# Ordering the second half of the last output product and the first products of a feed-forward as written

## The chip, the cores and the metric

The kernel runs on one core of a Trainium2 chip. A core has a matrix engine (TensorE: PE in the profile, its weight loads PEld), a vector engine (VectorE: DVE), a scalar engine (ScalarE: ACT), GpSimd (POOL) and a queue that issues DMAs (SP). Each takes its own instructions one after the other and waits for the others by semaphores. The metric is the device time of one execution in microseconds (us); less is better.

## The reference

One layer of a hybrid decoder, for 1024 tokens of width 1024, in float32. What matters here is its end:

```python
mixed = gates[:, :, 0] * y_ssm + gates[:, :, 1] * y_conv + gates[:, :, 2] * y_attn
x = x + mixed @ w_out[i]
h = rms_norm(x, ffn_norm_g[i])
f_gate, f_up = jnp.split(h @ ffn_w_gate_up[i], 2, axis=-1)
x = x + (jax.nn.silu(f_gate) * f_up) @ ffn_w_down[i]
```

`rms_norm` divides each token's row by the root of the mean of its squares and multiplies by a gain per column. `ffn_w_gate_up` is 1024 x 5632.

## The kernel before

Every product in float32 is made of three matmuls in the engine's faster float32 type: an operand is split into a high part (ACT copies it, L61) and the rest (DVE subtracts, L62), and high x high, high x low and low x high are added up in PSUM. On top of that the large products here use a Strassen scheme: 2 x 2 blocks and seven products in place of eight, with sums and differences of blocks as operands.

`out_rows` (from L1256) computes `mixed @ w_out` and adds it to x. Its seven products run in the order of `OUT`; each has four k-steps (`i`) and four token tiles (`t`), and one k-step of one tile is three matmuls (`mm`, L1282). A finished sum in PSUM is added to the tile's page x2 by DVE (`into`, L1290). The last product, number 4, is handled apart (from L1326): its loop has the tiles outside and the k-steps inside, and after each tile it finishes rows. `row` (L1294) takes one tile of 128 tokens: the sum of its squares (ACT, L219), the root (ACT, L209), the reciprocal (DVE, L210), the scaling (ACT for `act`, L213, else DVE, L215), and a DMA that keeps x2 in DRAM (L1297). Rows 0 to 3 are done during product 7, rows 4 to 7 here.

`quadrants` (L1364) turns four normalised rows into four blocks of 128 columns x 512 tokens: 16 transposes on PE (L1373) into two wide PSUM buffers, and four evictions, by ACT with the gain (L1379) or, where another operand is subtracted, by DVE (L1377). `operand_b` (L1393) splits such blocks. These are the right operands of the feed-forward's seven products: "11" and "21" come from rows 0 to 3, "T1" to "T4" and "22" need rows 4 to 7 too.

`ffn_up` (L1405) is a generator that yields at set places, so that `out_rows` can run it piece by piece with `next(up)`. Its list `flat` holds (i, z, p): a pair i of 128-column tiles of the weights, gate or up (z), the product p. It starts with products 1 and 2 of three pairs, which need right operands 11 and 21 alone. `operand(n)` splits the left operand of entry n from the raw weights (L61 and L62, tiles A), and for some entries starts the load of a later group (L1426). One product is twelve matmuls (L1517). Product 1 is copied from PSUM by ACT (L1520), and product 2 is added on top of it in the same bank:

```python
nc.tensor.matmul(ps, x, y, start=p in (1, 5, 6, 7) and k + j == 0, stop=k == 3 and j == 2,
```

After product 2 ACT applies SiLU for the gate (L1458), or DVE multiplies for the up part (L1462), from the same bank.

Which instruction stands where in an engine's queue is set by a planner: it walks through the program, lets each instruction in when its inputs, its tile's buffer and its engine are free by its own model of time, and gives the earlier one in the program the right of way. Inside `manual_schedule`, the named engines take their instructions in the order of the program. The kernel before uses that for PE in the state-space part alone (L1757); everything around the change is left to the planner. Buffers come from pools: 44 pages of 128 x 1024 floats, 14 of half that size, four PSUM banks and two wide PSUM buffers of two banks.

Of the kernel before, what the change touches and what calls it, by code (L numbers as in the profile page):

```python
# [12 lines left out]
OP = mybir.AluOpType  # L13
# [20 lines left out]
class Trunk:  # L34
# [554 lines left out]
    credit, t = 0.0, 0  # L589
# [666 lines left out]
    def out_rows(self):  # L1256
        nc = self.nc
        v = nc.vector
        x2, ss, xn = {}, self.const("ss2", [P, NT]), {}
        self.spill_x = self.dram.tile([S, D], F32, tag="sx", name="sx")  # L1260
        up = self.ffn_up()
        seq, parts = self.out_seq, {}

        def load(t):
            x2[t] = self.page("x2")
            nc.sync.dma_start(x2[t], self.i["x"][0, t * P:(t + 1) * P, :])

        def split(n):
            if n >= len(seq) or n in parts:
                return  # L1270
            p, i = seq[n]
            if n not in self.out_parts:
                self.out_right(n)
            r = self.left[i]
            if p in (1, 2):
                t = r.pop(p)
            else:
                t = self.page("lp", F32R)
                self.split(t[:, :512], t[:, 512:], r["src"].pop(p))
            parts[n] = t, self.out_parts.pop(n)  # L1280

        def mm(ps, n, t):  # L1282
            p, i = seq[n]
            act, w = parts[n]
            for j, (x, y) in enumerate(((0, 0), (0, 1), (1, 0))):
                nc.tensor.matmul(ps, act[:, x * 512 + t * P:x * 512 + (t + 1) * P], w[:, y * 512:y * 512 + 512],  # L1286
                                 start=i == 0 and j == 0 and p in (1, 5, 2), stop=i == 3 and j == 2,
                                 skip_group_check=True)

        def into(t, c, ps):  # L1290
            o = x2[t][:, c * 512:c * 512 + 512]
            v.scalar_tensor_tensor(o, ps, 0.5, o, op0=OP.mult, op1=OP.add)

        def row(t, act):  # L1294
            self.square_sum(x2[t], ss[:, t:t + 1])
            xn[t] = self.norm_row(x2[t], ss[:, t:t + 1], act)
            nc.sync.dma_start(self.spill_x[t * P:(t + 1) * P, :], x2[t])  # L1297
            del x2[t]
        INTO = {1: ((0, 0),), 2: ((0, 0),), 5: ((1, 1),), 6: ((0, 1),), 3: ((0, 1),), 7: ((1, 1),), 4: ((1, 0),)}
        for t in range(4):  # L1300
            load(t)
        first = [self.acc() for _ in range(4)]
        second = None
        for n, (p, i) in enumerate(seq[:-4]):
            if i == 0 and p in (5, 2):
                second = []
                for _ in range(2):
                    a = self.wide()
                    second += [a[:, :512], a[:, 512:]]
            if p == 2:  # L1310
                load(4 + i)
            for m in range(n, n + 3):
                split(m)
            for t in range(4):
                ps = (first if p in (1, 6, 7) else second)[t]
                mm(ps, n, t)
                if i == 3:
                    for h, c in INTO[p]:
                        into(4 * h + t, c, ps)
            del parts[n]  # L1320
            if p == 7 and i < 2:
                row(2 * i, 0)
                row(2 * i + 1, 0)
            if p == 7 and i == 0:
                next(up)
        n0 = len(seq) - 4  # L1326
        for n in range(n0, n0 + 4):
            split(n)
        self.B, half0 = {}, [xn.pop(j) for j in range(4)]
        q = self.quadrants(half0, 0)  # L1330
        for t in range(4):
            for n in range(n0, n0 + 4):
                mm(first[t], n, t)
            into(4 + t, 0, first[t])
            if t == 0:
                q += self.quadrants(half0, 4)
            elif t == 1:
                self.operand_b("11", q[:4])
                next(up)
            elif t == 2:  # L1340
                self.operand_b("21", q[4:])
            if t:
                row(3 + t, t % 2)
        row(7, 0)
        parts.clear()
        next(up)
        half1 = [xn.pop(4 + j) for j in range(4)]
        b11, b21 = q[:4], q[4:]
        t1 = self.quadrants(half1, 0, b11)
        self.operand_b("T1", t1)  # L1350
        next(up)
        b22 = self.quadrants(half1, 4)
        t2 = self.difference(v, b22, t1)
        self.operand_b("T2", t2)
        next(up)
        t3 = self.difference(v, t2, b11)
        self.operand_b("T3", t3)
        next(up)
        t4 = self.difference(v, b21, t2)
        self.operand_b("T4", t4)  # L1360
        self.operand_b("22", b22)
        self.run(up)
# [42 lines left out]
    def ffn_up(self):  # L1405

        nc = self.nc
        v = nc.vector
# [10 lines left out]
        def fetch(n):  # L1419
            if n < len(groups):  # L1420
                i, z, _ = groups[n]
                r = []
                for a in range(2):
                    t = self.page("raw")
                    c0 = z * D_FF + 2 * i * P
                    nc.sync.dma_start(t.rearrange("p (k c) -> p k c", k=4),  # L1426
                                      gu[4 * a * P:4 * (a + 1) * P, c0:c0 + 256].rearrange("(k p) c -> p k c", p=P))
                    r.append(t.rearrange("p (k f c) -> p k f c", k=4, f=2))
                raw[groups[n]] = r

        def operand(n):
            if n >= len(flat) or flat[n] in ops:
                return
            i, z, p = flat[n]
            g = i, z, int(i >= N or i > 0 and p not in (1, 2))
            if g[2] == 0 and p == 2 and i < N - 2:
                fetch(groups.index(g) + 4)
            elif p == 5:
                fetch(max(groups.index(g) + 2, 2 * N + z))
            lo, hi = raw[g]  # L1440
            a11, a21, a12, a22 = lo[:, :, 0], lo[:, :, 1], hi[:, :, 0], hi[:, :, 1]
            cut = lambda x: x.rearrange("p (k c) -> p k c", k=4)
            if p in (1, 2, 4):
                src = {1: a11, 2: a12, 4: a22}[p]
            else:
                src = cut(self.half("S"))
                x, y, op = {5: (a21, a22, OP.add), 6: (sums.get((i, z, 5)), a11, OP.subtract),
                            7: (a11, a21, OP.subtract), 3: (a12, sums.get((i, z, 6)), OP.subtract)}[p]
                v.tensor_tensor(src, x, y, op=op)  # L1449
                if p in (5, 6):  # L1450
                    sums[i, z, p] = src
            t = self.page("A", F32R)
            self.split(cut(t[:, :512]), cut(t[:, 512:]), src)
            ops[flat[n]] = t
# [32 lines left out]
            fetch(n)  # L1487
        yield
        for n in range(5):
            operand(n)  # L1490
        yield
        for n, (i, z, p) in enumerate(flat):
# [294 lines left out]
```

## Time and profile before

| | |
|---|---|
| three runs | 1752.97, 1753.34, 1754.22 us; median 1753.34 |
| the profiled execution's own time | 1753.43 us |
| its span, first to last instruction | 1751.5 us |
| granted TensorE clock, mean | 0.999 |
| transposes of the normalised rows (L1373) | 64, from 1086.5 to 1131.4 us |
| copies of product 1 (L1520) | 22, the first at 1107.6 us |

The span is shorter than the execution's own time by 1.9 us, which lie around it. The region that the change touches is that from 1086 to some 1158 us of the span.

### The profile page before, as it was taken

Reading aid. Unit: us, or ns where it says so; the run is one execution under the profiler, and the core shown is the slowest. Engines: PE = TensorE matmul, PEld = TensorE weight load, DVE = VectorE, ACT = ScalarE, POOL = GpSimd, SP = SyncE. Lnnn points to the kernel's source line nnn. Section 1 sums busy time; section 2 is a strip of 40 time slices with the busy share of each in tenths; the row PEclk is TensorE's granted clock in tenths of the full one; section 3 lists DMA queues with packets and bytes.
Section 4 is the critical chain, followed back from the end, with each engine's and each line's share of the span. In section 5 each row is a group of like instructions: output and inputs, shape, how many; then the busy total and the mean of one; then the engine's idle time right before and its main releaser. Section 6 shows DMA issues by size and latency. Waiting matters only on the chain.

```text
span 1751.5 us, 23611 instructions
## 1 busy us (share of the span) xinstructions
PE 1728.9 (99%) x8637; PEld 1433.2 (82%) x8637; DVE 1202.8 (69%) x2414; ACT 795.4 (45%) x1477; POOL 108.8 (6%) x94
## 2 busy tenths in 40 slices
PE   8999999999999999999999999999999999999999
PEld 8987788888888888888788888778888888888887
DVE  6975456667676664684685687798677776687681
ACT  7415566777777842333122244742222332344460
POOL 0000000000000010121000000011122111120000
PEclk9999999999999999999999999999999999999999
DMA  5213422221211125123566224333223332577521
GB/s 173 73 43 101 125 85 67 61 61 46 58 43 47 42 81 145 41 69 97 191 200 200 84 96 133 120 127 127 96 96 109 114 103 78 189 256 259 163 91 48
DMA packets 172664, 189.78 MB, mean 108 GB/s; under 512 B 16937, under 2 KB 129669, under 8 KB 172549
## 3 DMA queue, kind: packets, MB, share of 16 engines
q1 hardware_dynamic: 172517, 188.27, 33.5%
q8 instruction: 68, 1.11, 0.3%
q14 instruction: 47, 0.39, 0.1%
q10 hardware_dynamic: 32, 0.01, 0.0%
HBM read 134.50 MB, written 47.45 MB: 104 GB/s over the span
## 4 chain that ended last, share of the span: by engine, by line
PE 86%; DVE 6%; ACT 4%; issue 1%; DMA 1%; SPq 1%; POOL 0%; POOLq 0%; ACTq 0%; DVEq 0%
PE wide L1517 13%; PE acc L124 12%; PE acc L120 12%; PE acc L122 11%; PE acc L1517 9%; PE acc L1624 6%; PE wide L1624 5%; PE acc L560 3%; PE wide L519 3%; PE acc L1286 2%; PE wide L1286 2%; PE acc L583 2%; PE acc L582 2%; PE wide L257 1%; PE wide L256 1%
## 5 line engine op out<-in xcount | busy, mean ns | idle before, releaser
L120 PE MATMUL acc<-hh,whi 128*128 128x512 f32 x672 | 268.6, 400 | 1.5 <-DVE kl L66 1.5
L122 PE MATMUL acc<-hl,whi 128*128 128x512 f32 x672 | 267.9, 399 | 0.0
L124 PE MATMUL acc<-hh,wlo 128*128 128x512 f32 x672 | 267.4, 398 | 0.0
L1517 PE MATMUL wide<-B,A 128*128 128x512 f32 x1056 | 250.6, 391 | 0.3
L1517 PEld LDWEIGHTS wide<-B,A 128*128 128x128 f32 x1056 | 196.5, 188 | 47.0 <-DVE sg L1530 3.3
L1517 PE MATMUL acc<-B,A 128*128 128x512 f32 x792 | 190.6, 391 | 2.6 <-ACT A L61 1.6
L1517 PEld LDWEIGHTS acc<-B,A 128*128 128x128 f32 x792 | 147.9, 188 | 35.4 <-ACT A L61 2.5
L120 PEld LDWEIGHTS acc<-hh,whi 128*128 128x128 f32 x672 | 126.6, 188 | 22.3 <-issue 2.2
L122 PEld LDWEIGHTS acc<-hl,whi 128*128 128x128 f32 x672 | 126.7, 188 | 19.7 <-issue 0.2
L124 PEld LDWEIGHTS acc<-hh,wlo 128*128 128x128 f32 x672 | 126.8, 189 | 19.4 <-DVE wlo L62 0.4
L61 ACT ACTIVATE A<-S 128x512 fp32r<-128x512 f32 x88 | 54.8, 627 | 164.9 <-DVE S L1449 164.3
L62 DVE TENSOR_TENSOR ptl<-acc,pth 128x512 fp32r<-128x512 f32 (+1 forms) x152 | 93.8, 619 | 50.4 <-ACT pth L61 49.2
L1624 PE MATMUL acc<-wdp,act 128*128 128x512 f32 x528 | 121.5, 389 | 0.1
L524 DVE CUSTOM_DVE_ANT_0 p<-wide,mask 128x640 f32<-128x640 f32 (+7 forms) x128 | 90.1, 704 | 43.2 <-PE wide L519 40.5
L62 DVE TENSOR_TENSOR wlo<-raw,whi 128x1024 fp32r<-128x1024 f32 (+1 forms) x75 | 90.4, 1209 | 39.5 <-ACT whi L61 23.9
L1624 PEld LDWEIGHTS acc<-wdp,act 128*128 128x128 f32 x528 | 99.0, 188 | 21.2 <-DVE wdp L62 0.5
L1473 POOL TENSOR_TENSOR sg<-sg 128x512 f32<-128x512 f32 x44 | 73.9, 1679 | 590.3 <-ACT A L61 512.5
L527 ACT ACTIVATE p<-p,small 128x640 f32<-128x640 f32 (+7 forms) x128 | 93.6, 731 | 37.1 <-DVE small L524 35.1
L120 PE MATMUL acc<-mhi,whi 128*128 128x512 f32 x256 | 100.5, 392 | 1.8 <-DVE m L1166 1.8
L61 ACT ACTIVATE pth<-acc 128x512 fp32r<-128x512 f32 (+1 forms) x152 | 80.9, 534 | 46.0 <-PE acc L560 45.2
L124 PE MATMUL acc<-mhi,wlo 128*128 128x512 f32 x256 | 100.7, 393 | 0.3 <-DVE wlo L62 0.3
L122 PE MATMUL acc<-mlo,whi 128*128 128x512 f32 x256 | 100.5, 393 | 0.0
(397 smaller groups left out, 3246.1 us busy)
## 6 DMA issues: line engine op xcount, KB each, us to landing
raw<-in_ffn_w_gate_up_dram SPq DMA_DIRECT2D x52, 512.0 KB
raw<-in_w_in_dram SPq DMA_DIRECT2D x48, 512.0 KB
sa<-sg SPq DMA_DIRECT2D x77, 256.0 KB
araw<-sa SPq DMA_DIRECT2D x77, 256.0 KB
sg<-tg SPq DMA_DIRECT2D x48, 256.0 KB
gp<-sg SPq DMA_DIRECT2D x24, 512.0 KB
x<-in_x_dram SPq DMA_DIRECT2D x16, 512.0 KB
wd<-in_ffn_w_down_dram SPq DMA_DIRECT2D x11, 512.0 KB
```

What stands on the lines that cost most here:

```text
L61: self.nc.scalar.activation(hi, src, AF.Copy)
L62: self.nc.vector.tensor_tensor(lo, src, hi.bitcast(F32), op=OP.subtract)
L120: self.nc.tensor.matmul(out, hi(k), mh(k), start=start and j == 0, stop=False)
L122: self.nc.tensor.matmul(out, hi(k), ml(k), start=False, stop=False)
L124: self.nc.tensor.matmul(out, lo(k), mh(k), start=False, stop=stop and j == n - 1)
L519: nc.tensor.matmul(ps[:, c * 512:c * 512 + w], self.QS[t][:, h], k[:, k0 + c * w:k0 + c * w + w], start=z == 0, stop=z == 1)
L524: nc.vector.tensor_tensor_reduce(p[:, :n].rearrange("p (c w) -> p c w", c=pieces), v, m.rearrange("p (c w) -> p c w", c=pieces), scale=-1. ...
L527: nc.scalar.activation(p[:, :n], p[:, :n], AF.Exp, scale=-1.0, bias=st[:, hh:hh + 1], accum_out=st[:, 2 + hh:3 + hh])
L1286: nc.tensor.matmul(ps, act[:, x * 512 + t * P:x * 512 + (t + 1) * P], w[:, y * 512:y * 512 + 512], start=i == 0 and j == 0 and p in (1, 5, ...
L1473: e.tensor_tensor(o, x, y, op=op)
L1517: nc.tensor.matmul(ps, x, y, start=p in (1, 5, 6, 7) and k + j == 0, stop=k == 3 and j == 2, skip_group_check=True)
L1624: nc.tensor.matmul(ps, act[:, x * 512 + t * P:x * 512 + (t + 1) * P], w[:, y * 512:y * 512 + 512], start=i == 0 and j == 0 and p in (1, 5, ...
```

## The change

Three things change in the last product of `out_rows` and the start of `ffn_up`. The loop over the four tiles and what follows up to operand T1 stand in a `manual_schedule` for PE, DVE and ACT. Rows 5 and 7 take their sum of squares on DVE with one `tensor_tensor_reduce`; rows 4 and 6 keep ACT. And the order of the program is another: after the second tile come right operand 11, the left operands of entries 0 and 1, and right operand 21; after the third, rows 4 and 5; after the fourth, the left operands of entries 2 to 4, and rows 6 and 7. For this the generator yields once more, before entry 2. The loop that adds up products, its banks and the steps behind T1 stay as they were.

```diff
-        def row(t, act):
-            self.square_sum(x2[t], ss[:, t:t + 1])
+        def row(t, act, dve=False):
+            if dve:
+                v.tensor_tensor_reduce(self.page("junk"), x2[t], x2[t], scale=1.0, scalar=0.0, op0=OP.mult, op1=OP.add,
+                                       accum_out=ss[:, t:t + 1])
+            else:
+                self.square_sum(x2[t], ss[:, t:t + 1])
...
-        q = self.quadrants(half0, 0)
-        for t in range(4):
-            for n in range(n0, n0 + 4):
-                mm(first[t], n, t)
-            into(4 + t, 0, first[t])
-            if t == 0:
-                q += self.quadrants(half0, 4)
-            elif t == 1:
-                self.operand_b("11", q[:4])
-                next(up)
-            elif t == 2:
-                self.operand_b("21", q[4:])
-            if t:
-                row(3 + t, t % 2)
-        row(7, 0)
-        parts.clear()
-        next(up)
-        half1 = [xn.pop(4 + j) for j in range(4)]
-        b11, b21 = q[:4], q[4:]
-        t1 = self.quadrants(half1, 0, b11)
-        self.operand_b("T1", t1)
-        next(up)
+        E = mybir.EngineType
+        with self.tc.manual_schedule(engines={E.PE, E.DVE, E.Activation}):
+            q = self.quadrants(half0, 0)
+            for t in range(4):
+                for n in range(n0, n0 + 4):
+                    mm(first[t], n, t)
+                into(4 + t, 0, first[t])
+                if t == 0:
+                    q += self.quadrants(half0, 4)
+                elif t == 1:
+                    self.operand_b("11", q[:4])
+                    next(up)
+                    self.operand_b("21", q[4:])
+                elif t == 2:
+                    row(4, 1)
+                    row(5, 0, True)
+                else:
+                    next(up)
+                    row(6, 1)
+                    row(7, 0, True)
+            parts.clear()
+            next(up)
+            half1 = [xn.pop(4 + j) for j in range(4)]
+            b11, b21 = q[:4], q[4:]
+            t1 = self.quadrants(half1, 0, b11)
+            self.operand_b("T1", t1)
+            next(up)
...
         for n in range(5):
+            if n == 2:
+                yield
             operand(n)
```

## Rows read from the trace of the kernel before

**Rows 1.** The page's line of the span and its table of busy time by engine (us busy, share of the span, instructions).

```profile
span 1751.5 us, 23611 instructions
...
PE 1728.9 (99%) x8637; PEld 1433.2 (82%) x8637; DVE 1202.8 (69%) x2414; ACT 795.4 (45%) x1477; POOL 108.8 (6%) x94
```

**Rows 2.** The table of five stretches: busy us of PE, PEld, DVE, ACT and POOL, each with its number of instructions, then the granted clock, the share of the DMA engines and GB/s.

```profile
1086.46:1104.65 18.19, 18.09 (x94) 14.26 (x92) 14.40 (x24) 13.53 (x25) 0.00 (x0) 1.00 0.84 283
1104.65:1118.26 13.61, 13.61 (x62) 11.21 (x61) 5.64 (x11) 9.24 (x17) 0.00 (x0) 1.00 0.53 182
1118.26:1131.39 13.13, 10.92 (x62) 8.55 (x61) 10.80 (x18) 9.85 (x18) 0.00 (x0) 1.00 0.05 20
1131.39:1158.58 27.19, 25.55 (x111) 19.70 (x110) 26.88 (x46) 17.06 (x31) 0.00 (x0) 1.00 0.29 97
1158.58:1206.72 48.14, 48.14 (x214) 39.71 (x213) 41.80 (x58) 14.11 (x23) 9.54 (x6) 1.00 0.41 137
```

**Rows 3.** PE's instructions in order of time, 1074 to 1300 us, equal neighbours merged: start, us from the first's start to the last's end, engine, line, operation, output and input, shape, how many, and in brackets the idle time before and who ended it.

```profile
1086.46 0.60 PE L1373 MATMUL wide<-ident,xn 128*128 128x128 f32 x4
1086.82 3.00 PE L1286 MATMUL acc<-wop,lp 128*128 128x512 f32 x12
1089.66 0.60 PE L1373 MATMUL wide<-ident,xn 128*128 128x128 f32 x4
1090.02 3.82 PE L1286 MATMUL acc<-wop,lp 128*128 128x512 f32 x12
...
1097.09 0.66 PE L1373 MATMUL wide<-ident,xn 128*128 128x128 f32 x4
1097.50 0.48 PE L1286 MATMUL acc<-wop,lp 128*128 128x512 f32 x1
...
1104.65 13.77 PE L1517 MATMUL acc<-B,A 128*128 128x512 f32 x60
...
1120.27 0.44 PE L1373 MATMUL wide<-ident,xn 128*128 128x128 f32 x2 [1.20 <-DVE xn L215]
1121.71 3.08 PE L1517 MATMUL acc<-B,A 128*128 128x512 f32 x12 [1.00 <-ACT A L61]
...
1128.29 1.03 PE L1373 MATMUL wide<-ident,xn 128*128 128x128 f32 x8
...
1142.27 3.01 PE L1517 MATMUL acc<-B,A 128*128 128x512 f32 x12 [0.69 <-ACT p L1520]
...
1154.02 0.73 PE L1517 MATMUL acc<-B,A 128*128 128x512 f32 x2 [0.58 <-ACT A L61]
...
1156.18 2.56 PE L1517 MATMUL acc<-B,A 128*128 128x512 f32 x10 [0.38 <-DVE A L62]
```

**Rows 4.** ACT's instructions in the same form, 1070 to 1145 us.

```profile
1090.08 1.27 ACT L1379 ACTIVATE bq<-wide,gn 128x512 f32<-128x512 f32 x2 [0.95 <-PE wide L1373]
...
1107.57 0.60 ACT L1520 ACTIVATE p<-acc 128x512 f32<-128x512 f32 x1 [2.99 <-PE acc L1517]
...
1109.63 2.18 ACT L61 ACTIVATE B<-bq 128x512 fp32r<-128x512 f32 x4
1111.72 1.04 ACT L219 ACTIVATE junk<-x 128x1024 f32<-128x1024 f32 x1
1112.67 0.18 ACT L219 ACTIVATION_READ_ACCUMULATOR junk<-x 128x1 f32 x1
...
1113.24 0.28 ACT L209 ACTIVATE ss<-ss,eps 128x1 f32<-128x1 f32 x1
...
1115.12 1.15 ACT L213 ACTIVATE xn<-x,ss 128x1024 f32<-128x1024 f32 x1 [0.23 <-DVE ss L210]
```

**Rows 5.** One line of the source, L1373 (the transposes): how many, and the ns of one at least, in the middle and at most.

```profile
L1373 PE MATMUL wide<-ident,xn x64: 270/272/328, 1086.5 to 1131.4; 128*128 128x128 f32 x64
```

**Rows 6.** DVE's instructions in order of time, 1070 to 1145 us, in the form of rows 3.

```profile
1087.80 0.69 DVE L1292 SCALAR_TENSOR_TENSOR x<-acc,x 128x512 f32<-128x512 f32 x1 [3.23 <-PE acc L1286]
...
1095.28 0.68 DVE L62 TENSOR_TENSOR lp<-tgp,lp 128x512 fp32r<-128x512 f32 x1
...
1113.55 0.16 DVE L210 RECIPROCAL ss<-ss 128x1 f32<-128x1 f32 x1 [0.77 <-ACT ss L209]
1113.75 0.75 DVE L215 TENSOR_SCALAR xn<-x,ss 128x1024 f32<-128x1024 f32 x1
...
1123.58 1.40 DVE L1377 SCALAR_TENSOR_TENSOR bq<-wide,gn,bq 128x512 f32<-128x512 f32 x2
...
1126.60 2.49 DVE L62 TENSOR_TENSOR B<-bq,B 128x512 fp32r<-128x512 f32 x4
```

**Rows 7.** DVE's groups by line and shape: how many, then us in all and the mean ns of one, and the idle time before them. The first three are of the whole span, the last of 180 to 640 us, where the attention runs.

```profile
L62 DVE TENSOR_TENSOR wlo<-raw,whi 128x1024 fp32r<-128x1024 f32 x72 | 87.8, 1221 | 39.5 <-ACT whi L61 23.9 <-PE acc L122 10.7 <-ACT tg L672 2.5
...
L524 DVE CUSTOM_DVE_ANT_0 p<-wide,mask 128x1024 f32<-128x1024 f32 x8 | 9.8, 1224 | 3.9 <-PE wide L519 3.9
...
L62 DVE TENSOR_TENSOR mlo<-yT,mhi 128x1024 fp32r<-128x1024 f32 x4 | 8.1, 2029 | 2.0 <-ACT mhi L61 2.0
...
L524 DVE DVE_READ_ACCUMULATOR2_ANT small<- 128x1 f32 x128 | 10.6, 83 | 0.0
```

**Rows 8.** The issues on SP's queue in order of time, 1040 to 1145 us.

```profile
1079.66 8.80 SPq L1426 DMA_DIRECT2D raw<-in_ffn_w_gate_up_dram  x8
...
1100.53 2.61 SPq L1426 DMA_DIRECT2D raw<-in_ffn_w_gate_up_dram  x4
```

## The prediction

> **What bounds the kernel now.** I read the page first: TensorE (PE) is busy 99% of 1751.5 us, so only time in which PE stands still can be won, and any new stall of PE is paid in full [rows 1]. Then the table of stretches, to see where it stands still. The change touches about 1086 to 1158 us. PE has no idle time in the first two of these stretches beyond 0.1 us, 2.2 us in the third (13.13 less 10.92) and 1.64 us in the fourth, and afterwards it is dense (48.14 of 48.14 in the fifth) [rows 2]. So 3.85 us is all that shows as idle, and whatever delay or gain stands at 1158 us reaches the end. PE's order of time shows one more piece: twelve matmuls at 1090.02 took 3.82 us where twelve in a row take 3.00, so about 0.8 us is hidden there; with the 0.1 of the first stretch and small change I call it 0.65 to 1 [rows 3]. The ceiling of a gain is thus about 4.5 to 5 us, under 0.3%.
>
> The same view shows how the kernel fills PE today. Within L1286 and L1373, transposes stand in fours between matmuls, and 60 matmuls of the feed-forward's first five products run without a gap from 1104.65 [rows 3]. The code says why that is remarkable: product 2 adds to the same PSUM bank as product 1 (`start` is false for p == 2), so it can't begin before the copy of product 1 (L1520) has read the bank. The copy ran at 1107.57 for 0.60, when PE was inside the next product [rows 4]: the planner had put another product between. That such a wait is real is seen once at 1142.27, where PE stood 0.69 us for L1520 [rows 3].
>
> **The change, part by part.** The times below are on the clock of this profile. Unit prices: 60 matmuls in 13.77 us with a last one of 0.39 are 0.227 each, twelve 2.72; eight transposes in 1.03 with one of 0.27 are 0.11 each, sixteen 1.8 [rows 3, 5]. On DVE four splits in 2.49 with one of 0.68 are 0.60 apiece, and the sums into x2 (L1292) the same [rows 6]. On ACT four in 2.18 are 0.52 apiece [rows 4]. An eviction by ACT is 0.64, one by DVE 0.70 [rows 4, 6]. A hand-over between engines costs 0.03 (a root that ended at 1113.24 + 0.28 = 1113.52 was followed by its reciprocal at 1113.55 [rows 4, 6]); I use 0.04.
>
> (a) *Last output product as written.* PE must now run 16 transposes, then for the first sum all four k-steps, then 16 transposes, then the other three sums. Before, it took whichever step was split. The last pair's split ends on DVE at 1095.28 + 0.68 = 1095.96 [rows 6], so the first sum's last three matmuls run to 1095.96 + 0.68 = 1096.64. What follows is 1.8 + 36 x 0.227 = 9.96, to 1106.60, where before PE was through at 1104.65 [rows 3]: 1.95 us lost. From below: if the planner splits the pairs earlier, as ACT's halves would allow (DVE idles 3.23 us ahead of 1087.80 [rows 6]), nothing is lost and the hidden 0.65 comes back: -0.65. From above: one more pair of splits ahead of it, 2 x 0.60 late: +3.15. I take 1.95, since the splits are traced ahead of the block and nothing in it moves them.
>
> (b) *Vector queue as written, with two squares on it.* The second sum's addition (L1292) is now ahead of the right operands' splits in DVE's queue. It waits for PE: 1096.64 + 1.8 + 2.72 + 0.17 of pipeline = 1101.33. Behind it DVE never rests: addition 0.6, four B splits 2.4, two A 1.2, four B 2.4, addition 0.6 (7.2 so far); row 4's reciprocal 0.2, row 5's square 1.3, the wait for its root on ACT 0.4, reciprocal 0.2, scaling 0.7 (2.8); addition 0.6, three A 1.8 (2.4); row 6's reciprocal 0.2, row 7's square 1.3 (1.5). Sum 13.9, to 1115.25. Reciprocal and scaling are from their rows (0.16 and 0.75, 0.19 and 0.68 from start to next start) [rows 6]. The two-source reduction is in the trace for one PSUM and one SBUF source: 1224 ns for 128x1024 and 83 ns for its accumulator, 1.3 together [rows 7]. For two SBUF sources it is not shown; the nearest rows are 0.75 (the scaling of one source, [rows 6]) and 2.03 (a two-source instruction on a strided page, [rows 7]), which move the sum by -0.5 (one square is then hidden behind ACT) and by +1.5.
>
> (c) *ACT's queue.* The copy of product 1 is written behind row 7's root. ACT is ready for that root long before it comes: its own work from 1089 on is 8 evictions of 0.64, 13 splits of 0.52 and two rows of some 2.5 (square 1.04, accumulator 0.18, scaling 1.15), about 17 us, to 1106. But it can't pass it. Root at 1115.3, copy to 1116.05, product 2 from 1116.1. PE has ended product 1 at 1106.60 + 2.72 = 1109.32, so it stands 6.8 us. Queued behind the wait on PE are products 2 to 5, T1's transposes and two more products; on ACT the SiLU of product 2 and three splits. What could fill the hole is only later work outside the block: the 16 transposes for operand 22, when rows 4 to 7 are normalised; at most 1.8.
>
> (d) *Third to fourth product* has the same bank and nothing between: copy 0.60, its wait and the pipeline's end 0.24, 0.84 us. Fifth to sixth has T1's transposes between: nothing.
>
> (e) *What goes away.* Two squares of 1.04 and 0.18 leave ACT [rows 4], which costs or gives nothing by itself: ACT is hidden under the vector queue throughout. The five waits after 1118 us (1.20 for row 7's scaling, 1.00 for an A split behind a table load, 0.69, 0.58, 0.38 [rows 3]) are waits for DVE and ACT; PE arrives 1.95 + 6.8 + 0.84 = 9.6 us later. T1's transposes then begin at 1127.8; four DVE evictions (2.8) and four splits (2.4) end near 1133.7 against 1129.1 before [rows 6], 4.6 us later. The operands shift by half of what PE shifts by, so I count the whole 3.85 as regained. If nothing of it were, +3.85 more.
>
> (f) *SP's queue and pages.* The fetch of group 4 moves ahead of the spills, that of group 5 to the third step, near 1110; their pages are read by left operand 8 at some 1131 or later, 20 us on, and eight loads of the first groups were issued within 8.8 us [rows 8]. Zero; if that cover were gone, a load's few us would show at operand 8.
>
> Sum: 1.95 + 6.8 + 0.84 - 3.85 = +5.7 us. On the profiled execution's 1753.43 that is 1759.2, on the runs' median, 0.09 below it, 1759.1.
>
> [...]
>
> **Rivals.**
> [...]
> C, *a wash*: the planner's simulated order splits the pairs early (-2.6 against my term (a)) and puts the 16 transposes into the hole (-1.8): +1.3, 1754.7. For it: it did slip transposes into gaps before [rows 3]. Against: both must happen.
> D, *the order written is nearly the one already run*: 1753.3. Against: 60 matmuls without a gap can't be that order.
> E, *faster*: the strict order keeps up and lets DVE make right operands early. It decides at L1520's first copy: if that starts by 1109.5, no hole opens, (a) is at its lower end, and the 3.85 are won: 1753.3 - 4.5 = 1748.8. For it: ACT's own 17 us would be through by then. Against: DVE's 13.9 us can't begin before 1101.3, unless (a) is gone, and even then it ends at some 1112.7.
>
> **How the numbers follow.** The forecast has a chance of 0.53, B 0.10, C 0.18, D 0.05, E 0.14. A change under 0.2% (3.5 us, 1749.8 to 1756.8) can't be told from none here. So slower is 0.53 + 0.10 = 0.63, no change 0.18 + 0.05 = 0.23, faster 0.14. The forecast's own bounds are 1759.1 less 2.6 and 0.5, and plus 1.2 and 1.5: 1756.0 to 1761.8. The range reaches down past C and D to 1751.5 and up past B to 1762.5; E and little above are left out.
>
> **What would show it.** (a): PE waiting in L1286 for L62's last splits, some 2.5 us, and the first feed-forward product at 1106.6. (b): DVE idle ahead of L1292 near 1097 to 1101, then dense; two reductions of about 1.3. (c): L1520's first copy near 1115.4 and PE waiting 6 to 7 us for it. (d): a second wait of 0.8. (e): no waits of PE from there on, and the dense stretch that began at 1158.58 beginning some 5.7 later. I am wrong if PE runs into product 2 without a long wait, if it fills the hole with other products, or if new waits come behind the block.

## The result, and the profile after

The changed kernel takes 1765.16 us (median of six runs, 1762.86 to 1767.29) where the kernel before, run beside it, takes 1754.00 (1752.97 to 1755.01). The ratio is 1.0064, with a 95% interval of 1.0054 to 1.0074: it is slower, by 11.2 us. The forecast was slower by 5.7, and the time lies above its range. The profiled execution took 1765.61 us.

The page's lines of the span and of busy time, beside [rows 1]:

```profile
span 1763.7 us, 23612 instructions
...
PE 1731.4 (98%) x8637; PEld 1434.8 (81%) x8637; DVE 1205.7 (68%) x2418; ACT 793.9 (45%) x1473; POOL 108.1 (6%) x94
```

The span is 12.2 us longer, but PE's busy time only 2.5. The rest is PE standing still. The table of stretches says where, in the form of [rows 2] (busy us of PE, PEld, DVE, ACT, POOL, then granted clock, DMA share, GB/s); the cuts follow this kernel's own order:

```profile
1086.15:1109.25 23.10, 19.70 (x94) 15.84 (x92) 14.06 (x24) 14.45 (x27) 0.00 (x0) 0.93 0.71 240
1109.25:1118.31 9.06, 2.88 (x14) 2.07 (x12) 8.27 (x18) 6.21 (x12) 0.00 (x0) 0.90 0.68 228
1118.31:1126.37 8.06, 8.06 (x24) 6.10 (x24) 1.14 (x2) 2.36 (x3) 0.00 (x0) 0.69 0.01 4
1126.37:1136.65 10.28, 8.34 (x45) 6.62 (x45) 4.14 (x6) 3.93 (x7) 0.00 (x0) 1.00 0.07 27
1136.65:1168.66 32.01, 30.95 (x142) 24.43 (x140) 29.97 (x50) 21.33 (x39) 0.00 (x0) 1.00 0.25 82
1168.66:1218.00 49.34, 49.34 (x217) 40.73 (x218) 43.00 (x61) 14.11 (x23) 8.34 (x6) 1.00 0.39 128
```

The first row is the same work as the first row of [rows 2], the last output product with its transposes: 23.10 us against 18.19, with 3.40 idle where there was 0.1, and at a granted clock of 0.93. In the second PE works 2.88 of 9.06 us. In the third it is busy throughout, but at 0.69 of its clock. From the last row on it is dense again. Measured from the first transposes to the last wait before that dense part, the stretch is 1086.15 to 1168.66, 82.51 us; before it was 1086.46 to 1156.18, 69.72. The whole growth of the span (12.2) is in it; the region grew by 12.8, and 0.6 came back outside. I call it the region, and its length is the measure in every experiment below.

Two finer rows of the same view show that the granted clock was down to 0.51 twice:

```profile
1092.50:1096.00 3.50, 3.50 (x11) 2.85 (x11) 2.92 (x5) 0.69 (x1) 0.00 (x0) 0.51 0.93 326
...
1116.40:1123.30 6.90, 5.00 (x12) 3.93 (x13) 1.96 (x4) 3.13 (x4) 0.00 (x0) 0.51 0.29 111
```

In the second, twelve matmuls take 5.00 us, 0.42 each, where [rows 3] give 0.227.

PE's instructions in order of time, in the form of [rows 3] (L1382 are the transposes, L1528 the feed-forward's products, L1531 the copy of product 1, L1388 and L1386 the evictions by ACT and DVE):

```profile
1086.15 0.38 PE L1382 MATMUL wide<-ident,xn 128*128 128x128 f32 x2
...
1090.30 1.09 PE L1382 MATMUL wide<-ident,xn 128*128 128x128 f32 x8 [0.78 <-ACT bq L1388]
1092.31 0.93 PE L1382 MATMUL wide<-ident,xn 128*128 128x128 f32 x4 [0.92 <-ACT bq L1388]
1092.89 4.44 PE L1286 MATMUL acc<-wop,lp 128*128 128x512 f32 x12
1097.17 0.60 PE L1382 MATMUL wide<-ident,xn 128*128 128x128 f32 x4
1098.54 1.09 PE L1382 MATMUL wide<-ident,xn 128*128 128x128 f32 x8 [0.78 <-ACT bq L1388]
1100.56 0.66 PE L1382 MATMUL wide<-ident,xn 128*128 128x128 f32 x4 [0.92 <-ACT bq L1388]
1100.97 8.44 PE L1286 MATMUL acc<-wop,lp 128*128 128x512 f32 x36
1109.25 2.88 PE L1528 MATMUL acc<-B,A 128*128 128x512 f32 x12
1118.31 8.06 PE L1528 MATMUL acc<-B,A 128*128 128x512 f32 x24 [6.18 <-ACT p L1531]
1127.06 5.74 PE L1528 MATMUL acc<-B,A 128*128 128x512 f32 x24 [0.69 <-ACT p L1531]
...
1134.07 1.09 PE L1382 MATMUL wide<-ident,xn 128*128 128x128 f32 x8 [0.84 <-DVE bq L1386]
1135.58 1.31 PE L1382 MATMUL wide<-ident,xn 128*128 128x128 f32 x8 [0.41 <-DVE bq L1386]
...
1155.68 3.01 PE L1528 MATMUL acc<-B,A 128*128 128x512 f32 x12 [0.69 <-ACT p L1531]
...
1168.66 2.57 PE L1528 MATMUL acc<-B,A 128*128 128x512 f32 x10 [0.37 <-DVE A L62]
```

Here stand three kinds of loss. Four waits of the transposes for ACT's evictions, 0.78 and 0.92 twice over, 3.40 in all (e2_apart below shows that the first two cost little by themselves): a wide buffer holds two blocks, and PE begins the second only when the first has been evicted. The planner had kept fours of transposes between matmuls, so that the eviction fell beside them [rows 3]. Then the hole of 6.18 us behind product 1. And matmuls that are busy for too long at a lower clock: twelve in 4.44 at 1092.89 (0.51 up to 1096.00), and 24 in 8.06 behind the hole (0.69).

What led to the hole, on DVE and on ACT:

```profile
1094.73 0.69 DVE L62 TENSOR_TENSOR lp<-tgp,lp 128x512 fp32r<-128x512 f32 x1
...
1104.01 0.69 DVE L1292 SCALAR_TENSOR_TENSOR x<-acc,x 128x512 f32<-128x512 f32 x1 [5.95 <-PE acc L1286]
...
1111.30 1.21 DVE L1296 CUSTOM_DVE_ANT_0 junk<-x 128x1024 f32<-128x1024 f32 x1
1112.43 0.09 DVE L1296 DVE_READ_ACCUMULATOR2_ANT ss<- 128x1 f32 x1
...
1116.22 1.21 DVE L1296 CUSTOM_DVE_ANT_0 junk<-x 128x1024 f32<-128x1024 f32 x1
1117.36 0.08 DVE L1296 DVE_READ_ACCUMULATOR2_ANT ss<- 128x1 f32 x1
```

```profile
1111.42 1.15 ACT L213 ACTIVATE xn<-x,ss 128x1024 f32<-128x1024 f32 x1 [2.91 <-DVE ss L210]
...
1117.47 0.29 ACT L209 ACTIVATE ss<-ss,eps 128x1 f32<-128x1 f32 x1
1117.67 0.58 ACT L1531 ACTIVATE p<-acc 128x512 f32<-128x512 f32 x1
```

DVE waits 5.95 us for the second sum, then works without a gap of more than 0.4 from 1104.01 to 1117.44. Row 7's square is the last of it, ACT's root follows 0.03 later, and the copy of product 1, for which PE has stood since 1112, is next in ACT's queue. ACT itself had waited 2.91 for row 4's reciprocal.

### The profile page after: what moved, and what is told of

Same layout as the page of the kernel before. It is cut to its first block, busy times and chain, and to the rows that moved or that the text cites. A ratio compares the mean times of both kernels' runs of the same rounds, so it can differ in the third digit from the quotient of the medians.

```text
span 1763.7 us, 23612 instructions
## 1 busy us (share of the span) xinstructions
PE 1731.4 (98%) x8637; PEld 1434.8 (81%) x8637; DVE 1205.7 (68%) x2418; ACT 793.9 (45%) x1473; POOL 108.1 (6%) x94
## 4 chain that ended last, share of the span: by engine, by line
PE 86%; DVE 6%; ACT 4%; issue 1%; SPq 1%; DMA 1%; ACTq 0%; DVEq 0%
PE wide L1528 13%; PE acc L120 11%; PE acc L124 11%; PE acc L122 11%; PE acc L1528 8%; PE acc L1635 7%; PE wide L1635 5%; PE acc L560 3%; PE wide L519 3%; PE acc L1286 2%; PE wide L1286 2%; PE acc L583 2%; PE acc L582 2%; PE wide L257 1%; PE wide L256 1%
## 5 line engine op out<-in xcount | busy, mean ns | idle before, releaser
L1528 PE MATMUL wide<-B,A 128*128 128x512 f32 x1056 | 250.5, 391 | 0.3
L1528 PEld LDWEIGHTS wide<-B,A 128*128 128x128 f32 x1056 | 196.6, 188 | 46.8 <-DVE sg L1541 3.3
L1528 PE MATMUL acc<-B,A 128*128 128x512 f32 x792 | 192.3, 394 | 7.9 <-ACT p L1531 7.6
L1528 PEld LDWEIGHTS acc<-B,A 128*128 128x128 f32 x792 | 149.7, 190 | 41.0 <-ACT p L1531 9.0
```

## The experiments

Eleven kernels were run, each beside the kernel before on the same chip (its medians there: 1753.4 to 1753.8). The region's difference is against 69.72 us.

| kernel | median us | ratio (95%) | region |
|---|---|---|---|
| the change | 1765.16 | 1.0064 (1.0054 to 1.0074) | +12.8 |
| e1_planner | 1750.95 | 0.9983 (0.9974 to 0.9993) | -2.3 |
| e2_apart | 1755.84 | 1.0014 (1.0005 to 1.0023) | +2.8 |
| e3_swap | 1762.44 | 1.0048 (1.0033 to 1.0063) | +9.5 |
| e4_warm | 1761.45 | 1.0043 (1.0026 to 1.0060) | +9.1 |
| e5_pe_only | 1757.05 | 1.0017 (1.0007 to 1.0026) | +5.0 |
| e6_dve_act_only | 1757.01 | 1.0017 (1.0008 to 1.0026) | +5.5 |
| e7_squares_alone | 1753.61 | 0.9999 (0.9990 to 1.0008) | -0.2 |
| e8_planner_apart | 1750.87 | 0.9986 (0.9977 to 0.9994) | -1.5 |
| e9_planner_squares_act | 1752.96 | 0.9998 (0.9989 to 1.0006) | -0.7 |
| e10_apart_swap | 1753.60 | 1.0002 (0.9993 to 1.0012) | +0.7 |
| e11_planner_late_pair | 1750.52 | 0.9981 (0.9972 to 0.9990) | other order |

**The queues given back to the planner.** All else as in the change.

```diff
-        with self.tc.manual_schedule(engines={E.PE, E.DVE, E.Activation}):
+        with ExitStack():
```

> The changed kernel without the order as written: squares on DVE and the new order of the program stay, the planner places everything. Theory (the fixed order costs the whole 11 us): within 3 us of the kernel before, 1751 to 1757, products without the long gap behind the first, transposes again in small groups between matmuls, granted clock at 1.00 from 1086 to 1158 us. Rival (the squares on DVE or the new order of the program cost it): 1760 or more.

It is 14.2 us faster than the change and 2.9 faster than before. The waits of PE from 1103.81 to the end of the region:

```profile
1107.38 11.27 PE L1528 MATMUL acc<-B,A 128*128 128x512 f32 x48 [0.69 <-ACT p L1531]
...
1139.76 3.01 PE L1528 MATMUL acc<-B,A 128*128 128x512 f32 x12 [0.69 <-ACT p L1531]
...
1153.06 2.58 PE L1528 MATMUL acc<-B,A 128*128 128x512 f32 x10 [0.37 <-DVE A L62]
```

So the loss belongs to the order as written. The new order of the program and the squares on DVE, planned, leave 1.75 us of waits where before there were 3.85 [rows 3]: the waits for row 7's scaling (1.20) and for A splits (1.00, 0.58) are gone, and one for the copy of product 1 has come.

**The products of one bank apart.** The first five products run in the order 1, 3, 5, 2, 4 of the list, so product 1's copy has two products' time before it is needed.

```diff
+        flat[:5] = [flat[0], flat[2], flat[4], flat[1], flat[3]]
```

> The changed kernel with its first five products in the order 1, 3, 5, 2, 4 (numbers of the list), so that a product 1 is never followed by the product 2 of the same bank. Theory (PE stands for the copy of product 1, and the clock falls because it stands): the 6.3 us behind the first product shrink to some 3 us (the left operand of the next one comes late from DVE), the 0.85 us behind the third go, and 1758 to 1762 us come out, at the lower end if the clock doesn't fall. Rival (PE is held by the queues of ACT and DVE as a whole, whatever the product): the gap stays above 5 us, 1764 to 1766.

PE, below it the stretch from the first transposes to the first product (columns as above), and the last weight load of the first sum:

```profile
1091.38 1.09 PE L1382 MATMUL wide<-ident,xn 128*128 128x128 f32 x8 [0.78 <-ACT bq L1388]
1093.39 0.66 PE L1382 MATMUL wide<-ident,xn 128*128 128x128 f32 x4 [0.92 <-ACT bq L1388]
1093.81 3.25 PE L1286 MATMUL acc<-wop,lp 128*128 128x512 f32 x12
...
1108.97 8.42 PE L1529 MATMUL acc<-B,A 128*128 128x512 f32 x36
1118.03 5.73 PE L1529 MATMUL acc<-B,A 128*128 128x512 f32 x24 [0.64 <-ACT p L1532]
```

```profile
1087.23:1108.97 21.74, 18.34 (x93) 14.55 (x92) 14.05 (x24) 14.49 (x27) 0.00 (x0) 1.00 0.60 204
```

```profile
1096.55 0.19 PEld L1286 LDWEIGHTS acc<-wop,lp 128*128 128x128 f32 x1 [0.40 <-DVE lp L62]
```

The hole is 0.64 us instead of 6.18, and the 24 matmuls behind it take 5.73 instead of 8.06. The time is 9.3 us under the change and 2.2 under the theory's lower end: the left operand, for which 3 us had been left, was not late. In the profiles the regions differ by 9.9: 5.54 is the hole, 2.33 the slow matmuls behind it, 0.69 the wait of the second pair, and 1.36 lies in the first stretch. There the transposes' waits are unchanged, yet this execution kept the clock at 1.00; the stretch is 3.55 over before, against 4.91 in the change. That 1.36 is the price of the clock's first fall: the same stretch takes 21.74 in e4_warm, without the fall, and 23.10 in e5_pe_only, with it. And at a clock of 1.00 the first sum still ends on the last split, as the weight load's wait shows: the first two waits of the transposes, 1.70, are hidden ahead of it.

**The transposed blocks in the order 0, 2, 1, 3**, so that neighbours lie in different wide buffers. Each block keeps its page and its buffer.

```diff
-        for k in range(k0, k0 + 4):
+        for k in (k0, k0 + 2, k0 + 1, k0 + 3):
...
```

> The changed kernel with the four transposed blocks taken in the order 0, 2, 1, 3, so that two in a row go to different wide PSUM buffers; same work. Theory (a block waits until the other half of the same wide buffer has been evicted): the waits of about 0.8 and 0.9 us in each set of sixteen shrink by two thirds; the first set gains little, since the last split then holds the first sum; the second and third gain about 1.3 and 0.8; 1761 to 1763. Rival (a block waits for the eviction of the block before it, whatever the buffer): same waits, 1764 to 1766.

```profile
1090.14 1.24 PE L1384 MATMUL wide<-ident,xn 128*128 128x128 f32 x8 [0.34 <-ACT bq L1390]
...
1093.51 2.31 PE L1286 MATMUL acc<-wop,lp 128*128 128x512 f32 x5 [0.51 <-DVE wop L62]
1095.65 1.03 PE L1384 MATMUL wide<-ident,xn 128*128 128x128 f32 x8
1097.03 1.24 PE L1384 MATMUL wide<-ident,xn 128*128 128x128 f32 x8 [0.34 <-ACT bq L1390]
...
1115.35 8.34 PE L1530 MATMUL acc<-B,A 128*128 128x512 f32 x24 [6.17 <-ACT p L1533]
```

The waits of the transposes fall from 3.40 to 0.68: it is the other half of the same buffer that PE waits for. Whether the two halves could be told apart by the program's own bookkeeping was not tried. Now PE reaches the split of the last pairs too early: 0.51 for wop, and five matmuls that take 2.31 instead of some 1.3 (four at 0.227 and a last one of 0.39 [rows 3], an estimate). So the first set gains nothing, and the second set, 3.80 us in the change from 1097.17 to 1100.97, takes 2.37 from 1095.65 to 1098.02. First transposes to first product is 1085.99 to 1106.30, 20.31 us, 2.12 over before and 2.79 under the change; 1.36 of that is the first fall of the clock, which this execution did not have. The hole stays 6.17 long, and the clock behind it falls as in the change: it was 0.67 from 1113.40 to 1123.69, and the 24 matmuls took 8.34.

**Work for PE in the hole.** 24 further matmuls behind product 1, whose result nobody reads; all of the computation is still there.

```diff
+            if n == 0:
+                warm, b = self.wide(), B[0]
+                for _ in range(24):
+                    nc.tensor.matmul(warm[:, :512], b[:, :P], b[:, :512], start=True, stop=True)
```

> The changed kernel with 24 matmuls more behind the first product, which fill 5.4 of the 6.3 us for which PE stands; they write to a wide PSUM buffer that nobody reads. Theory (the clock falls because PE stood): the granted clock stays at 1.00 there, the products that ran at 0.427 us a matmul run at 0.227, and 2.5 us go in spite of more work: about 1762.7. Rival (the fall has another cause, or costs nothing at the end): 1765 or more.

```profile
1110.50 5.60 PE L1533 MATMUL wide<-B 128*128 128x512 f32 x24
1116.84 5.74 PE L1528 MATMUL acc<-B,A 128*128 128x512 f32 x24 [0.74 <-ACT p L1535]
```

```profile
1116.84:1122.58 5.74, 5.74 (x24) 4.42 (x24) 1.14 (x2) 2.36 (x3) 0.00 (x0) 1.00 0.02 9
```

Product 2 still waits for the same copy, but the 24 matmuls behind the wait run at a clock of 1.00 and take 5.74 instead of 8.06 us: 2.3 us is what PE's standing still for 6.18 costs here beyond its length. The other executions bear it out: the mean granted clock is 0.996 to 0.998 in the change's six and 0.999 to 1.000 in e4_warm's four. With work that does nothing the kernel is 3.7 us faster than the change. In the two profiled executions 1.4 of that is the first fall, which this one did not have, though its transposes wait 0.78 and 0.92 as in the change.

**PE alone, and DVE and ACT alone, as written.**

```diff
-        with self.tc.manual_schedule(engines={E.PE, E.DVE, E.Activation}):
+        with self.tc.manual_schedule(engines={E.PE}):
```

> The changed kernel with the order as written for PE alone; DVE and ACT are placed by the planner. Theory (the long gap comes from the copy of product 1 standing behind the last row in ACT's queue): ACT's queue now has that copy ahead of row 6, so the 6.3 us become some 2 us, the clock stays up behind it, and the waits of the transposes for their evictions, which PE's order alone makes, stay at about 2 us in each of the first two sets: 1757 to 1760. Rival (PE's order alone makes the gap): over 5 us of it stay, 1763 to 1766.

```diff
-        with self.tc.manual_schedule(engines={E.PE, E.DVE, E.Activation}):
+        with self.tc.manual_schedule(engines={E.DVE, E.Activation}):
```

> The changed kernel with the order as written for DVE and ACT alone; PE is placed by the planner. Theory (PE's order makes the transposes' waits, the queues of DVE and ACT delay the copy): no waits inside the sets of transposes, but still a gap of some us where PE waits for the first copy or for the left operand behind it; 1754 to 1758, no fall of the clock if the gap stays under 4 us. Rival (DVE's and ACT's order costs nothing without PE's): as with the planner for all, 1750 to 1752.

With PE alone (the transposes' four waits and the clock's first fall are there as in the change), the clock's first fall and the wait behind product 1:

```profile
1093.90:1097.40 3.50, 3.50 (x11) 2.92 (x12) 3.08 (x6) 0.69 (x1) 0.00 (x0) 0.51 0.97 338
```

```profile
1114.37 5.74 PE L1528 MATMUL acc<-B,A 128*128 128x512 f32 x24 [0.69 <-ACT p L1531]
```

With DVE and ACT alone as written, PE planned, and below it the window behind that wait:

```profile
1108.32 0.44 PE L1382 MATMUL wide<-ident,xn 128*128 128x128 f32 x2 [2.00 <-ACT xn L213]
```

```profile
1108.90:1115.70 6.80, 6.57 (x16) 4.85 (x17) 5.16 (x10) 5.67 (x10) 0.00 (x0) 0.50 0.78 251
```

The hole takes both halves of the order. If ACT may take the copy when PE is through, product 2 waits 0.69; if PE may take something else first, the planner puts transposes there, and these wait 2.00 for row 4. Behind that wait the clock falls too, to 0.50, against the expectation: its 4 us fit the change, where the clock was still 1.00 after PE had stood for 4.2 us (1112.10 to 1116.30), and did not hold here.

Beside the kernel before, either half costs 3.3 us and all three queues 11.2. But the program is e1_planner's, which is 2.9 under before, and from there the halves cost 6.2 and 6.1 and the whole 14.0. The 1.8 us by which the whole exceeds the sum are no more than the intervals leave open (some 1.7 us each), and by the region it is 7.3 and 7.8 against 15.1. The two halves add up, though the losses are not the same ones: the long hole needs both, and with DVE and ACT alone another wait and another slow stretch come in its place.

**The squares alone**, in the kernel before.

```diff
-                row(3 + t, t % 2)
-        row(7, 0)
+                row(3 + t, t % 2, t == 2)
+        row(7, 0, True)
```

> The kernel before with one thing changed: the sums of squares of rows 5 and 7 on DVE. Theory (the gain of the planner-placed version over the kernel before comes from the squares leaving ACT, which had row 7 late by 1.2 us and the split behind it by 1.0): 1750.5 to 1752. Rival (it comes from the new order of the program): 1753.5 to 1755.

No change in the time, as the rival had it. PE's waits of 1.20 and 1.00 become one, behind the transposes:

```profile
1122.03 3.10 PE L1521 MATMUL acc<-B,A 128*128 128x512 f32 x12 [2.23 <-ACT A L61]
```

**Three variants of the planned kernel.** First e1_planner with the apart order, e2's line:

```diff
+        flat[:5] = [flat[0], flat[2], flat[4], flat[1], flat[3]]
```

> No order as written, squares on DVE, the new order of the program, and the first five products in the list order 1, 3, 5, 2, 4. Theory (the one wait left among these products, 0.69 us for the copy of the first, goes): 1750.2, 0.7 under the planner-placed version. Rival (the planner had that wait for want of an operand, or another takes its place): 1751, no difference.

Then e1_planner with all squares on ACT:

```diff
-                    row(5, 0, True)
+                    row(5, 0)
...
-                    row(7, 0, True)
+                    row(7, 0)
```

> No order as written, the new order of the program, all sums of squares on ACT as in the kernel before. Theory (the 2.9 us by which the planner-placed version beats the kernel before need the new order of the program and not the squares on DVE, since the squares alone gave nothing): 1750.5 to 1752. Rival (they need both): 1753 to 1755.

Last e1_planner with two later products exchanged, to free the wait at 1139.76:

```diff
+        flat[11], flat[12] = flat[12], flat[11]
```

> No order as written, squares on DVE, the new order of the program, and entries 11 and 12 of the product list exchanged, so that the last product 2 on a bank isn't next to its product 1. Theory (PE's wait of 0.69 us there is for the copy alone): 1750.3, 0.7 under the planner-placed version. Rival (operand T1, the next product's left operand or a wide buffer is late instead): 1751 to 1752.

The apart order gains nothing there, as the rival had it: 60 matmuls run without a gap again, but waits of 0.30, 0.27 and 0.72 come behind them. Without DVE's squares the kernel is level with before (0.4 under it, within the interval), again the rival's side. So the gain of e1_planner shows only with the new order and the squares together; each alone is worth nothing that can be measured. The exchange removes its 0.69 wait from the trace, but no gain shows in the time: e11_planner_late_pair is 2.8 us under the runs of before beside it, as e1_planner is 2.9 under those beside it.

**Both repairs of the order as written**, e2's and e3's.

```diff
-        for k in range(k0, k0 + 4):
+        for k in (k0, k0 + 2, k0 + 1, k0 + 3):
...
+        flat[:5] = [flat[0], flat[2], flat[4], flat[1], flat[3]]
```

> The order as written for PE, DVE and ACT, with both rearrangements: first five products in the list order 1, 3, 5, 2, 4, transposed blocks in the order 0, 2, 1, 3. Theory (what the fixed order costs is these waits, and they add up): 1755.8 from the products' order less the 2.7 that the blocks' order gave, 1753.1, level with the kernel before. Rival (the gain of the second is eaten, since the left operands of the later products then hold PE): 1755 to 1756.

```profile
1115.26 5.76 PE L1531 MATMUL acc<-B,A 128*128 128x512 f32 x24 [0.63 <-ACT p L1534]
```

1753.60, level with before, as the theory had it. With the two causes removed nothing of the loss is left, and nothing of e1_planner's gain appears: three queues as written can be made as good as the planner's order in the kernel before, here no better.

## Why the prediction went wrong

The direction and the largest stall were right; the sum was half of what came. Two things failed. The clock was put at nothing, without a reason: the slow matmuls behind the hole cost 2.46 us, and the clock's first fall 1.36 of the first stretch. And the transposes were priced without a wait between their blocks, which missed 1.60 in (a) and 1.25 at T1. By the prediction's steps, with the region's account:

| step | predicted | found |
|---|---|---|
| (a) last output product | +1.95 | +4.91 |
| (c) hole behind product 1 | +6.8 | +6.18 |
| slow matmuls behind the hole | not in the sum | +2.46 |
| (d) third to fourth product | +0.84 | +0.69 |
| T1's transposes | 0 | +1.25 |
| (e) idle time regained | -3.85 | -2.79 |
| sum | +5.7 | +12.7 |

The found figures are the first stretch less 18.19; the bracket at 1118.31; 8.06 less 5.60 for 24 matmuls at full clock; the bracket at 1127.06; 0.84 + 0.41; and 3.85 less the 0.69 and 0.37 that stayed. The region itself grew by 12.79.

(a) is short by 2.96. Of that 1.36 is the clock's first fall, by e2_apart; the other 1.60 is its price of the transposes. "Then 16 transposes", at 1.8 for sixteen, took their duration from a trace in which the planner had spread them among matmuls, and I did not ask what the second block of a buffer waits for once all sixteen stand together. The answer was in the code: `two` serves two blocks. It is the second set that costs: 3.80 us from 1097.17 to 1100.97 where I had 1.8; the first sum, at a clock of 1.00, ends some 0.4 sooner than I had it. The term that I did price, the wait for the last pair's split, was sound: in e2_apart and e4_warm the first sum ends on it, with the first set's waits hidden ahead of it, and in e3_swap the stretch is 2.12 over before. In the change the clock's fall covers it: the split ended at 1095.42, and the twelve slow matmuls ran beyond it, to 1097.33. The same omission stands in (d), "Fifth to sixth has T1's transposes between: nothing": there the evictions are DVE's, and the waits 1.25.

(b) held. DVE's line was worked out as 13.9 us and took 13.4; it began 2.7 later than I had it, since (a) was late. The two-source reduction took 1.21 with 0.09 for its accumulator, against 1.3. How much of the hole the two squares make is not shown: the order as written was not run with all squares on ACT. Both sources stood in SBUF, and the 1.21 is no more than the 1.22 of the traced one of [rows 7]. No run shows the slower square that stands behind the chance of B and the upper end of the range.

(c) held in its chain and, within 0.6, in its length (root 1117.47, copy 1117.67); its two ends were both over 2 us later than I had them, since (a) was. The hole is the largest single loss. What was missing behind it is a term of its own: the clock. PE stood still for 6.18 us, the granted clock fell to 0.51 before product 2 began (from 1116.40 on), and its first twelve matmuls took 5.00 us. e4_warm shows it apart from the wait. I had written of PE only that idle time is paid in full; here it is paid more than in full.

(d) measured 0.69 for 0.84. (e) was too generous: two waits late in the region, 0.69 for a copy and 0.37 for a split, came back at their old size. I had counted both as waits that a late PE no longer meets. But the copy follows PE's own product 1 in the same bank, so it is as late as PE: the 0.69 stands in every profile except e11_planner_late_pair's, where another product comes between. The split stands on DVE, which had worked from 1143.63 on without a wait of note, and was late by as much too. (f) held: no wait for a load shows in the region.

Of the rivals, C and D needed PE to find other work in the hole, or the order to be nearly the old one; the trace shows neither. E named the point that decides, the first copy by 1109.5, and it came at 1117.67.

## What to carry to other kernels

Before an order of queues is fixed by hand, list for each instruction what it waits for when its neighbours are no longer between: the halves of a shared PSUM buffer (3.40 us of waits in the change's first two sets of transposes), and two products in one bank with a copy between them (6.18, 0.69 and 0.69). When PE and the engines that feed it are all held in order, one engine's late row stops a copy that another engine's next instruction needs, and neither can go round it: product 2 waited 6.18 us so, and 0.69 with PE alone as written. Compare such an order with the same program under the planner, and not with the kernel before alone: here that turns a loss of 11 us into one of 14. And price a hole of several us in TensorE with the slow matmuls that may stand behind it: 2.46 us behind the 6.18 here.

## What was not expected of the hardware

A hole of PE was followed by a lower clock in three kernels (the change, e3_swap, e6_dve_act_only), behind waits of 6.18, 6.17 and 2.00 us: 0.51 from 1116.40 to 1123.30, 0.67 from 1113.40 to 1123.69 and 0.50 from 1108.90 to 1115.70. But e7_squares_alone waited 2.23 at 1122.03 and ran on at 1.00 (its twelve matmuls took 3.10). These are single profiles. The first fall, to 0.51 at 1092.5 in the change and at 1093.9 in e5_pe_only, stood behind waits of 0.78 and 0.92 with transposes between; it shows in the profiles of these two, and not in those of e2_apart and e4_warm, which have the same waits. Another such difference lies where no kernel is changed: from 844 to 855 us the granted clock was 0.84 in the profiles of before and of e2_apart and 1.00 in those of the change and of e1_planner. Here is that stretch in before, and below it in the change, with 34 and 40 matmuls:

```profile
844.00:855.00 11.00, 9.19 (x34) 7.10 (x33) 10.97 (x22) 1.06 (x1) 0.00 (x0) 0.84 1.04 394
```

```profile
844.00:855.00 11.00, 9.18 (x40) 7.05 (x39) 10.97 (x22) 1.06 (x1) 0.00 (x0) 1.00 1.03 397
```

The executions of one kernel differ in the same way. Of the 79 of before that ran beside the experiments, 32 had a mean granted clock of 1.000 and took 1752.69 us on average, and 46 had 0.999 and took 1754.09: 1.40 more, about the 1.36 that the first fall costs. So a difference of that size between two single profiles need not belong to the kernel; why a fall comes in one execution and not in another is open.
